# A decoder layer on one core: a product that alternates between two kinds of head, an earlier load, other buffer starts and other due times

## The chip, the cores and the metric

The kernel runs on one core of one Trainium2 chip. A run's time is the device time of the launch in microseconds (us). Three runs of the kernel before took 3005.85, 3009.3 and 3020.05 us, a median of 3009.3 us. The profile is of one more execution, of 3014.2 us.

## The reference

One layer of a decoder, in fp32, over 2048 tokens of width 1024: an RWKV-7 mixer with 16 heads of 64, a layer norm, an FFN of width 2816 with a causal convolution of width 3 and a gate, and a second layer norm.

```python
r = xr @ w_rkv[0]; k = xk @ w_rkv[1]; v = xv @ w_rkv[2]      # token shift mixes x and its predecessor
decay = exp(-exp(-softplus(-(w0 + tanh(xw @ w1) @ w2)) - 0.5))
a = sigmoid(a0 + (xa @ a1) @ a2); gate = sigmoid(xg @ g1) @ g2
def step(state, inp):                                         # for each of 2048 tokens, 16 heads, 64 x 64
    sa = einsum('bhij,bhj->bhi', state, -kk_t)
    state = state * w_t + sa x (kk_t * a_t) + v_t x k_t
    return state, einsum('bhij,bhj->bhi', state, r_t)
x = layer_norm(ALPHA * x + ((head_norm(y) + bonus) * gate) @ w_o)
hdn = conv(x @ w_in) + conv_b;  u, g = split(hdn)
out = layer_norm(ALPHA * x + (silu(g) * u) @ w_out)
```

## The kernel before

Four stages follow each other and overlap a little at their seams: the projections (0 to about 715 us, `a_nodes`), the recurrence (about 695 to 1285 us, `s_nodes`), the output projection with the first norm (about 1275 to 1520 us, `w_nodes`), and the FFN with the second norm (about 1500 us to the end, `f_nodes`).

**Large products.** A product of the projections, the output projection or the FFN is made of three TensorE matmuls of 128x512: each operand is split into a rounded part (H) and the rest (L), and HH, HL and LH are accumulated (`mm3`, L162 to L164 in the profile). In the names, `ps<-WH,xiH` reads: into `ps`, from the moving tile `WH` (512 columns) and the stationary tile `xiH` (128x128). In the FFN `ps<-xH,wiH` has x moving and the weights stationary, and `acc<-woH,aH` is the second product. Each matmul loads its stationary tile anew, beside the matmul ahead of it.

**Buffers.** Each pool is wrapped in `Pool64`, which rounds a tile's size in each partition up to 64 bytes. Where a tile begins in its partition, in bytes modulo 256, follows from the sizes of what lies in front of it. In the built program the large products' tiles begin at these remainders:

| matmuls | moving tile at | stationary tile at |
|---|---|---|
| projections, second column half (h=1): 1152 | 32 | 32 |
| projections, first column half (h=0): 1152 | 224 | 32 |
| FFN, first product: 4224 | 160 | 224 |
| FFN, second product: 2064, by the buffers | 32 | 32 or 224 |
| of these the last of the last block | 224 | 224 |

**Recurrence.** The 2048 steps are done in 16 chunks t of 128 tokens, each of two halves c of 64. Heads go in eight pairs p of two (e = 0, 1), which lie in partitions 0 to 63 and 64 to 127. For a chunk, loads (`th`, `rk`, `bk`), decays (`csI`, `P`, `Pi`), transposes (`tr`, `tb`, `pcp`) and Gram products `G` come first; DVE masks them into `Gm`. Part of `Gm` goes to DRAM (`NU`) and comes back as `NUs`; a table of identities comes from DRAM as `XU`; on these, DVE solves 32x32 triangular systems in 31 pairs of instructions (`itmp` and `XU`, L976 and L981), in place. `mp` merges two 32x32 solutions into one of 64x64. The part that goes from half to half is: `Z` (from `UV`, `Gm` and `state`), ACT copies it to `Zs`, `SA`, ACT copies it to `UV`, `dS`, then DVE forms `stmp` and `state` (L1129, L1134). `Z`'s second step (`f_z2`) has two matmuls for each pair p: one for e=1 that reads `state` and uses a 64x64 corner of the array, and one for e=0 that reads `SZ` and uses 128 rows and 64 columns. Before, the eight of the first kind come ahead of the eight of the second. From t=12 on the pairs are taken in two groups of four. These matmuls are in full fp32 and each shows as two passes in the profile (256 matmuls of a kind, 512 rows).

**Order.** All work is handed to a list scheduler (`Plan`). Each node has an engine, an estimated duration, a due time (`prio`, the smaller first), the nodes that it needs, and buffer slots. The plan writes down one order for each engine, and an engine runs its instructions in that order, waiting at the first that isn't ready. Due times are offsets in the tables `TS` (recurrence) and `TW` (output projection): for a chunk t, `b = t * T`, and `hs`, `cs`, `lds`, `inv` and so on are added to it. All loads named here go through SyncE's one DMA queue (SP).

Of the kernel before, what the change touches and what calls it, by code (L numbers as in the profile page):

```python
# [11 lines left out]
F32 = mybir.dt.float32  # L12
# [8 lines left out]
T, D, FF = 2048, 1024, 2816  # L21
# [11 lines left out]
    return bass.AP(tensor=ap.tensor, offset=ap.offset, ap=[[0, n], [1, ap.shape[-1]]])  # L33


class Pool64:


    def __init__(self, pool):
        self.pool = pool  # L40

    def tile(self, shape, dtype, **kw):
        n = math.prod(shape[1:])
        if n % 16 == 0:
            return self.pool.tile(shape, dtype, **kw)
        x = self.pool.tile([shape[0], -(-n // 16) * 16], dtype, **kw)[:, 0:n]
        if len(shape) > 2:
            d = " ".join(f"d{i}" for i in range(1, len(shape)))
            x = x.rearrange(f"p ({d}) -> p {d}", **{f"d{i}": shape[i] for i in range(2, len(shape))})
        return x  # L50
# [84 lines left out]
class K:  # L135
# [3 lines left out]

    def pool(self, st, **kw):  # L140
        p = st.enter_context(self.tc.tile_pool(**kw))
        return p if kw.get("space") is not None else Pool64(p)

    def ld(self, out, in_):
        return self.nc.sync.dma_start(out, in_)  # L145
# [1 line left out]
    st = ld  # L147
# [18 lines left out]
    def rsqrt(self, pool, out, x, n, m=None):  # L166

        nc = self.nc
        w = pool.tile([128, n], F32, name="rsw", bufs=1)[:, 0:m or n]
        y = pool.tile([128, n], F32, name="rsy", bufs=1)[:, 0:m or n]  # L170
        nc.vector.tensor_scalar(w.bitcast(I32), x.bitcast(I32), 1, None, op0=OP.arith_shift_right)
        nc.vector.tensor_scalar(y.bitcast(I32), w.bitcast(I32), -1.0, float(0x5F3759DF), op0=OP.mult, op1=OP.add)
        for i in range(3):
            nc.vector.tensor_tensor(w, y, y, op=OP.mult)
            nc.vector.scalar_tensor_tensor(w, w, -0.5, x, op0=OP.mult, op1=OP.mult)
            nc.vector.scalar_tensor_tensor(out if i == 2 else y, w, 1.5, y, op0=OP.add, op1=OP.mult)


    def run(self, phases="ASWF", scratch=None):
        tc, nc, a = self.tc, self.nc, self.a  # L180
        with ExitStack() as ctx:
            dram = ctx.enter_context(tc.tile_pool(name="dram", bufs=1, space=DRAM))
            self.S = {}
            mk = scratch or (lambda shape, name: dram.tile(shape, F32, name=name))
            for t in range(NT):
                for q in ("vc", "Y"):
                    self.S[q, t] = mk([128, D], f"{q}_{t}")
                self.S["gs", t] = mk([128, 2, D], f"gs_{t}")
                for h in range(2):

                    s = mk([129, 5, 512], f"in_{t}_{h}")
                    self.S["in", t, h] = s[1:129]
                    for i, q in enumerate(("r", "kkn", "b", "kp", "th")):
                        self.S[q, t, h] = s[0:128, i] if q == "kkn" else s[1:129, i]
                    self.S["kk0", t, h] = s[128:129, 1]
                    c = slice(h * 512, h * 512 + 512)
                    for q in ("vc", "Y"):
                        self.S[q, t, h] = self.S[q, t][:, c]
                    self.S["gateg", t, h] = self.S["gs", t][:, 0, c]
                    self.S["svbg", t, h] = self.S["gs", t][:, 1, c]  # L200
            self.x1T = [dram.tile([128, KD, 512], F32, name=f"x1T_{b}") for b in range(T // 512)]
            self.xn1 = [dram.tile([128, D], F32, name=f"xn1_{t}") for t in range(NT)]
            self.NU = [dram.tile([64, 1024], F32, name=f"NU_{t}") for t in range(NT)]
            self.XD = [dram.tile([64, 1024], F32, name=f"XD_{t}") for t in range(NT)]
            top = ctx.enter_context(tc.tile_pool(name="top", bufs=1))

            self.ident = top.tile([128, 136], F32, name="ident")[:, 8:136]
            self.ld(self.ident, a["c_ident"])
            self.build(ctx, phases)
            for n in self.plan.order():  # L210
                n.fn()

    def build(self, ctx, phases):
        ctx.enter_context(self.tc.manual_schedule())
        fs = {**self.TW["slots"], **self.TF["slots"]}
        fa = dict(self.TA["slots"])
        for h in range(2):
            fa.update({f"W{h}{k}": 1 for k in range(KD)})
        pl = self.plan = Plan({**fa, **self.TS["slots"], **fs}, fifo={*fa, *fs} - {"pg0", "pg1"})
        n_1, n_2 = self.a_nodes(ctx, pl) if "A" in phases else (None, None)  # L220
        pl.off = self.TS["p0"] + 23 * self.TA["g"] if "A" in phases else 0.0
        if "S" in phases:
# [6 lines left out]
    def a_nodes(self, ctx, pl):  # L229
# [56 lines left out]
        for sw, (q, wi, mm, ml) in enumerate((("k", 1, 2, 4), ("r", 0, 0, 1), ("v", 2, 3, 5))):  # L286
# [271 lines left out]
            for nq, (g, h, tl) in enumerate(order):  # L558
# [190 lines left out]
        return n_1, n_2  # L749


    TS = dict(hf=12, T=23.2, lds=5.0, hs=8.9, inv=31.0, mrg=66.3, mc=4.0, uv=47.5, st=70.2, cs=17.6, e0=30.0, p0=-3.4, fill=(), fn=1,
              slots=dict(cs=1, lth=1, lrk=1, lbk=1, pw=4, P=1, Pi=1, AR=4, BKn=4, Gm=4, PC=4, BKT=2, NUs=2, XU=2, XT0=1, XT1=1, X11=2, mp=1,
                         FT=2, UV=2, c0=1, c1=1, Y=1, Yt=1))

    def s_nodes(self, ctx, pl, n_1, n_2, w, f):

        tc, nc, a = self.tc, self.nc, self.a
        o = self.TS
        sl = o["slots"]  # L760
# [51 lines left out]
        inv = wkp = ldp = pw = triI = gmask = cols = gm4 = nbI = nbIn = nbE = scE = None  # L812
        cst = wk = ch2 = sm = pm = pc = None
        chs, XTs, SV, ZS, SW, V, SZ, n_za = [None] * sl["AR"], [], {}, {}, {}, {}, [], []
        n_o1 = pl.add("-", 0, 0, f_open1, [n_1])
        n_o2 = pl.add("-", 0, 0, f_open2, [n_o1, n_2])
        n_z2 = pl.add("POOL", 4.0, -9.0, f_zero2, [n_o2], lat=0.2)
        n_c = pl.add("SP", 2.0, -8.5, f_c, [n_o1])

        def tile_of(t, name, pool, shape, **kw):  # L820
            V[t][name] = pool.tile(shape, F32, name=name if isinstance(name, str) else name[0], **kw)
            return V[t][name]

        prevS, prevA, prevY = [], None, None
        for t in range(NT):
            v = V[t] = {}
            b = t * o["T"]
            P = lambda off, b=b: b + off
            grams, pcs, ars = [], [], {}
            for h in range(2):  # L830
                hb = b + h * o["hs"]
# [15 lines left out]
                n_lt = pl.add("SP", 1.0, lb - 0.3, f_lt, [n_o1], take=("lth",), lat=2.5)  # L847
# [2 lines left out]

                def f_cs(t=t, h=h):
                    MM(tile_of(t, ("csI", h), pw, [128, 512], tag="pw"), triI, V[t]["th", h])
                n_ci = pl.add("PE", 0.86, hb, f_cs, [n_lt] + [n_c] * (t == 0), take=("cs", "pw"), give=("lth",))

                def f_P(t=t, h=h):
                    P = tile_of(t, ("P", h), wkp, [128, 2, 512], tag="P", bufs=sl["P"])
# [7 lines left out]
                            nc.scalar.activation(x[es(part), c], V[t]["csI", h][es(c)], AF.Exp, bias=nbIn[es(c)],  # L864
                                                 scale=CDEC)
                n_P = pl.add("ACT", 1.24, hb + 0.2, f_P, [n_ci], take=("P",))
                n_Pi = pl.add("ACT", 2.4, hb + 0.4, f_Pi, [n_ci, n_P], take=("Pi",), give=("cs", "pw"))

                def f_alloc(t=t):
                    tile_of(t, "AR", chs[t % len(chs)], [128, 2, 8, 2, 64])  # L870
# [77 lines left out]
            e0 = (t == 0) * o["e0"]  # L948
            ib = b + o["inv"] - e0
# [15 lines left out]
                self.ld(x.rearrange("q m t -> q (m t)"), a["c_xui"])  # L965
            n_nu = pl.add("SP", 2.0, ib, f_nu, grams, lat=2.5)
            n_ns = pl.add("SP", 1.0, ib, f_nus, [n_nu], take=("NUs",), lat=3.0)
            n_xu = pl.add("SP", 1.0, ib, f_xu, [n_nu], take=("XU",), lat=2.5)
            prev = [n_ns, n_xu]
            for s in range(31):  # L970
                m, n = s // 2 + 1, 31 - s
# [21 lines left out]
            for c in range(2):  # L993
                mc = mb + o["mc"] * c
# [46 lines left out]
                n = pl.add("DVE", 0.93, mc, f_x11, [n_xt], take=("X11",))  # L1041
                n_m1 = pl.add("PE", 0.62, mc, f_m1, [n], take=("mp",), give=("X11",))
                n = pl.add("ACT", 0.79, mc, f_ft, [n_m1], take=("FT",), give=("mp",))
                n = pl.add("PE", 0.62, mc, f_m2, [n], take=("mp",), give=("FT",))
# [10 lines left out]
            for c in range(2):  # L1055
# [22 lines left out]
                for u in range(nh):  # L1078
                    ps = range(8 // nh * u, 8 // nh * (u + 1))
# [18 lines left out]
                    def f_z2(t=t, c=c, ps=ps, H=H, i0=i0):  # L1098
                        for p in ps:
                            MM(H["Z"][64:128, p], V[t]["AR"][64:128, c, p, 0], SV[i0][64:128, p], start=False,  # L1100
                               stop=p == ps[-1])
                        for p in ps:
                            MM(H["Z"][0:64, p], V[t]["AR"][:, c, p, 0], SZ[0][:, p], start=False, stop=p == ps[-1])

                    def f_zs(H=H, sl8=sl8, u=u, i0=i0):
# [25 lines left out]
                    def f_s1(t=t, c=c, u=u, sl8=sl8, i0=i0, i1=i1, n=ps[-1] + 1 - ps[0]):  # L1131
                        if u == 0:
# [15 lines left out]
                              give=("AR", "BKn", "Gm", "PC", "UV") if c else ())  # L1148
# [16 lines left out]
        for t0, t1, dt in o["fill"]:  # L1165
            n = pl.add("-", 0, 0, lambda: None, lat=t0)
            for i in range(int((t1 - t0) / dt)):
                pl.add("PE", 0.22 * o["fn"], 500 + i, f_fill, [n], take=("mp",), give=("mp",))
                n = pl.add("-", 0, 0, lambda: None, [n], lat=dt)
        if w:  # L1170
# [1 line left out]
                         pl.add("-", 0, 0, pools2.close, stores), stores, f)  # L1172


    TW = dict(ne=4, st=-31.5, gt=-31.1, tr=-14.5, ld=-22.0, out=26.9, p0=1000.0,
              slots=dict(w_ygE=2, w_gsE=2, w_yg=3, w_gs=4, w_xt=4, w_q=4, w_y=2, w_pwE=1, w_pwL=3, w_pzE=3, w_pzL=1,
                         w_xn=2, w_xo=2, w_st=2))

    def w_nodes(self, ctx, pl, n_first, n_ch1, xds, Q, n_rest, stores, f):

        tc, nc, a = self.tc, self.nc, self.a
        o = self.TW
        sl = {k[2:]: v for k, v in o["slots"].items()}
# [255 lines left out]
    def f_nodes(self, ctx, pl, Q, n_early, n_w, n_rest, zs, gn, n_sx, n_x1):  # L1439
# [51 lines left out]
        TAG = {"pz": "z", "pw": "tr"}  # L1491
        bank = lambda kind, i: kind + ("E" if i % 4 < self.TW["slots"][f"w_{kind}E"] else "L")
        pu = [0]
# [303 lines left out]
```

## Time and profile before

| | |
|---|---|
| median of 3 runs | 3009.3 us (3005.85 to 3020.05) |
| profiled execution | 3014.2 us, of which the span of the trace 3012.4 us |
| mean granted TensorE clock | 0.976 |
| TensorE busy | 2878.5 us (96%) |
| VectorE busy | 2018.5 us (67%) |
| ScalarE busy | 1693.5 us (56%) |

Busy shares are means over the four stages; in each of them another engine can be near its limit. A matmul's busy time in the profile is modelled, and neighbours overlap: what a matmul costs in a stream is the distance from its start to the next one's start. Rows that merge several instructions show how many (x16) and the start of the first.

### The profile page before, as it was taken

The numbers are of one execution on the slowest core, as the hardware profiler recorded it, in microseconds if no ns is written. First come the engines' busy times: TensorE is split into PE (matmuls) and PEld (weight loads), VectorE is DVE, ScalarE is ACT, GpSimd is POOL, SyncE is SP. The second block draws the span as 40 slices with busy tenths as digits, with TensorE's granted clock in tenths as the row PEclk, the third lists the DMA queues.
The fourth block names the chain that finished last, engine by engine and source line by source line (L and its number), as shares of the span: only waits on it lengthen the run. The fifth ranks groups of instructions, "written<-read, shape, count | busy, mean of one in ns | idle before, by whom it ended". The sixth has DMA issues, their size and how long they took to land.

```text
span 3012.4 us, 53465 instructions
## 1 busy us (share of the span) xinstructions
PE 2878.5 (96%) x20416; PEld 2342.4 (78%) x20416; DVE 2018.5 (67%) x4032; ACT 1693.5 (56%) x4580; POOL 53.5 (2%) x95
## 2 busy tenths in 40 slices
PE   7998999998899989989999999999999999999997
PEld 5776778886677877868888887878888788887886
DVE  7888769976877878678765555474554745547454
ACT  8888657655666766667554444434444344443441
POOL 0000000001000000001100000000000000000000
PEclk9999999999899999899999999999999999999999
DMA  6346555336666766468552334343243432434322
GB/s 204 138 165 232 174 182 195 142 117 178 158 154 155 173 156 142 127 229 284 191 182 89 95 97 124 96 143 96 88 126 95 144 95 89 133 95 143 91 84 81
DMA packets 283313, 428.12 MB, mean 142 GB/s; under 512 B 122448, under 2 KB 148048, under 8 KB 283056
## 3 DMA queue, kind: packets, MB, share of 16 engines
q1 hardware_dynamic: 271728, 383.81, 42.7%
q0 software_dynamic: 11328, 40.90, 3.7%
q8 instruction: 160, 2.62, 0.4%
q14 instruction: 97, 0.79, 0.1%
HBM read 315.50 MB, written 109.12 MB: 141 GB/s over the span
## 4 chain that ended last, share of the span: by engine, by line
issue 55%; PE 24%; ACT 7%; DMA 6%; DVE 6%; POOL 1%; SPq 1%; POOLq 0%; DVEq 0%; ACTq 0%
PE ps L162 4%; PE ps L163 4%; PE ps L164 4%; ACT junk L641 3%; PE Z L766 2%; DMA XU<-in_c_xui_dram 2%; PE G L766 1%; PE Y L766 1%; SPq L145 1%; PE csI L766 1%; ACT Pi L864 1%; DVE itmp L976 1%; DMA stg<-in_w_rkv_dram 1%; DVE XU L981 1%; PE dS L766 1%
## 5 line engine op out<-in xcount | busy, mean ns | idle before, releaser
L162 PE MATMUL ps<-xH,wiH 128*128 128x512 f32 x1408 | 557.2, 396 | 0.0
L164 PE MATMUL ps<-xH,wiL 128*128 128x512 f32 x1408 | 556.7, 395 | 0.5 <-DVE wiL L1585 0.3
L163 PE MATMUL ps<-xL,wiH 128*128 128x512 f32 x1408 | 556.6, 395 | 0.0
L1585 DVE TENSOR_TENSOR wiL<-wis,wiH 128x1024 fp32r<-128x1024 f32 x176 | 215.3, 1223 | 497.6 <-ACT wiH L1446 497.6
L1446 ACT ACTIVATE hb<-ps 128x512 f32<-128x512 f32 x176 | 105.6, 600 | 523.2 <-PE ps L164 523.2
L162 PE MATMUL ps<-WH,xiH 128*128 128x512 f32 x768 | 307.2, 400 | 15.6 <-ACT xiH L253 10.1
L164 PEld LDWEIGHTS ps<-xH,wiL 128*128 128x128 f32 x1408 | 264.7, 188 | 65.3 <-DVE wiL L1585 1.8
L163 PEld LDWEIGHTS ps<-xL,wiH 128*128 128x128 f32 x1408 | 264.9, 188 | 63.5
L162 PEld LDWEIGHTS ps<-xH,wiH 128*128 128x128 f32 x1408 | 264.8, 188 | 62.6
L163 PE MATMUL ps<-WL,xiH 128*128 128x512 f32 x768 | 304.7, 397 | 2.0 <-DVE WL L348 2.0
L164 PE MATMUL ps<-WH,xiL 128*128 128x512 f32 x768 | 304.4, 396 | 0.0
L163 PE MATMUL acc<-woL,aH 128*128 128x512 f32 x688 | 272.2, 396 | 9.8 <-DVE woL L1550 9.8
L1613 DVE SCALAR_TENSOR_TENSOR cv<-hb,cw,cv 128x512 f32<-128x512 f32 x352 | 263.6, 749 | 21.9 <-ACT cv L1609 15.7
L164 PE MATMUL acc<-woH,aL 128*128 128x512 f32 x688 | 272.1, 396 | 0.0
L162 PE MATMUL acc<-woH,aH 128*128 128x512 f32 x688 | 269.8, 392 | 0.0
L1446 ACT ACTIVATE wiH<-wis 128x1024 fp32r<-128x1024 f32 x178 | 189.0, 1062 | 11.9 <-DMA wis<-in_w_in_dram 11.9
L162 PEld LDWEIGHTS ps<-WH,xiH 128*128 128x128 f32 x768 | 146.5, 191 | 55.7 <-ACT xiH L253 10.1
L1446 ACT ACTIVATE woH<-wos 128x512 fp32r<-128x512 f32 x172 | 108.3, 632 | 123.5 <-PE acc L164 121.1
L163 PEld LDWEIGHTS ps<-WL,xiH 128*128 128x128 f32 x768 | 146.5, 191 | 35.0 <-DVE WL L348 2.5
L164 PEld LDWEIGHTS ps<-WH,xiL 128*128 128x128 f32 x768 | 146.1, 190 | 33.6 <-DVE xiL L472 0.2
L163 PEld LDWEIGHTS acc<-woL,aH 128*128 128x128 f32 x688 | 130.1, 189 | 42.0 <-DVE woL L1550 12.5
L976 DVE TENSOR_TENSOR itmp<-XU,NUs 128x126 f32<-128x126 f32 (+21 forms) x496 | 119.6, 252 | 55.3 <-DMA XU<-in_c_xui_dram 45.3
(244 smaller groups left out, 5294.2 us busy)
## 6 DMA issues: line engine op xcount, KB each, us to landing
wis<-in_w_in_dram SPq DMA_DIRECT2D x176, 512.0 KB
wos<-in_w_out_dram SPq DMA_DIRECT2D x172, 256.0 KB
xT<-in_xT_dram SPq DMA_DIRECT2D x21, 1028.0 KB
in<-kp SPq DMA_DIRECT2D x64, 256.0 KB
rk<-in SPq DMA_DIRECT2D x32, 512.0 KB
bk<-in SPq DMA_DIRECT2D x64, 256.0 KB
stg<-in_w_rkv_dram SPq DMA_DIRECT2D x48, 256.0 KB
gs<-gs SPq DMA_DIRECT2D x24, 512.0 KB
```

Source lines behind the costliest of these rows:

```text
L145: return self.nc.sync.dma_start(out, in_)
L162: nc.tensor.matmul(ps, lH, rH, start=start, stop=False)
L163: nc.tensor.matmul(ps, lH, rL, start=False, stop=False)
L164: nc.tensor.matmul(ps, lL, rH, start=False, stop=stop)
L641: nc.scalar.activation(junk, Z["kr"][:, 64 * i:64 * i + 64], AF.Square, accum_out=st["ss"][:, tl, i:i + 1])
L766: MM = lambda out, l, r, **kw: nc.tensor.matmul(out, l, r, **{**dict(start=True, stop=True), **kw}, skip_group_check=True)
L864: nc.scalar.activation(x[es(part), c], V[t]["csI", h][es(c)], AF.Exp, bias=nbIn[es(c)], scale=CDEC)
L976: TT(V[t]["tv"], V[t]["XU"][:, 0:m, s:s + 1].to_broadcast([128, m, n]), V[t]["NUs"][:, s:s + 1, s + 1:32].to_broadcast([128, m, n]), op=OP ...
L981: TT(x, x, V[t]["tv"], op=OP.add)
L1446: CP = lambda out, in_, **kw: nc.scalar.activation(out, in_, AF.Copy, **kw)
L1585: TT(W["L"], W["s"], W["H"], op=OP.subtract)
L1613: STT(R[j], W["hb"][:, i:i + 512], C["cw"][:, fc, i:i + 1], R[j], op0=OP.mult, op1=OP.add)
```

## The change

1. In `f_z2` the two matmuls of a pair p now follow each other, so that the kinds alternate eight times.
2. The load of `XU` (identities) needs only that its pool is open, and is due 12 units earlier. Before, it needed `NU`'s store, and so the Gram products.
3. `Pool256` takes the place of `Pool64`. It rounds sizes so that the buffers of one tile all begin alike modulo 256, and `ident` begins 64 bytes later in its tile, which is 64 bytes longer. In the built program every 128x512 matmul of the large products then has its stationary and its moving tile at remainder 224.
4. Other numbers in `TS` and `TW`, and two other estimated durations (`n_ci`, `n_Pi`).

```diff
-class Pool64:
+class Pool256:
-    def __init__(self, pool):
-        self.pool = pool
-    def tile(self, shape, dtype, **kw):
+    def __init__(self, pool, bufs):
+        self.pool, self.bufs = pool, bufs
+    def tile(self, shape, dtype, bufs=None, **kw):
+        b = bufs or self.bufs
         n = math.prod(shape[1:])
-        if n % 16 == 0:
-            return self.pool.tile(shape, dtype, **kw)
-        x = self.pool.tile([shape[0], -(-n // 16) * 16], dtype, **kw)[:, 0:n]
+        u = 64 // math.gcd(64, 16 * b) * 16 if n % 64 else 64
+        if n % u == 0 or n % 64 == 0:
+            return self.pool.tile(shape, dtype, bufs=b, **kw)
+        x = self.pool.tile([shape[0], -(-n // u) * u], dtype, bufs=b, **kw)[:, 0:n]
...
-            self.ident = top.tile([128, 136], F32, name="ident")[:, 8:136]
+            self.ident = top.tile([128, 152], F32, name="ident")[:, 24:152]
...
-    TS = dict(hf=12, T=23.2, lds=5.0, hs=8.9, inv=31.0, mrg=66.3, mc=4.0, uv=47.5, st=70.2, cs=17.6, e0=30.0, p0=-3.4, fill=(), fn=1,
+    TS = dict(hf=12, T=26.16, lds=5.61, hs=9.77, inv=31.0, mrg=66.3, mc=4.0, uv=47.5, st=70.2, cs=20.21, e0=30.0, p0=-3.4, fill=(), fn=1,
...
-            n_xu = pl.add("SP", 1.0, ib, f_xu, [n_nu], take=("XU",), lat=2.5)
+            n_xu = pl.add("SP", 1.0, ib - 12, f_xu, [n_o1], take=("XU",), lat=2.5)
...
                         for p in ps:
                             MM(H["Z"][64:128, p], V[t]["AR"][64:128, c, p, 0], SV[i0][64:128, p], start=False,
                                stop=p == ps[-1])
-                        for p in ps:
                             MM(H["Z"][0:64, p], V[t]["AR"][:, c, p, 0], SZ[0][:, p], start=False, stop=p == ps[-1])
...
-    TW = dict(ne=4, st=-31.5, gt=-31.1, tr=-14.5, ld=-22.0, out=26.9, p0=1000.0,
+    TW = dict(ne=4, st=-23.31, gt=-28.94, tr=-23.33, ld=-22.89, out=30.7, p0=1000.0,
```

The first place is TensorE's order around `f_z2` in the first half of chunk 5 (`Z<-state` and `Z<-SZ` are its two kinds; a row with x8 is eight matmuls in a row). Before:

```order
3096 L766 MATMUL Z<-UV,Gm 64x64 x16
3097 L766 MATMUL Y_11063<-UV,Gm 64x64 x16
3098 L766 MATMUL Z<-state,AR 64x64 x8
3099 L766 MATMUL Z<-SZ,AR 64x64 x8
3100 L766 MATMUL mp<-X_11260,Gm 32x32 x16
3101 L766 MATMUL Y_11307<-state,AR 64x64 x16
```

And after, at the same place, the start of the block and its end:

```order
3235 L768 MATMUL Y_11264<-state,AR 64x64 x16
3236 L768 MATMUL Z<-state,AR 64x64
3237 L768 MATMUL Z<-SZ,AR 64x64
3238 L768 MATMUL Z<-state,AR 64x64
3239 L768 MATMUL Z<-SZ,AR 64x64
...
3251 L768 MATMUL Z<-SZ,AR 64x64
3252 L768 MATMUL mp<-XT_7824,FT 32x32 x16
3253 L768 MATMUL SA<-Zs,XT_7824 64x64 x16
```

Two runs of eight became sixteen single matmuls of changing kind; `Y<-state` moved from behind the block to ahead of it, and 16 `mp` stand between the block and `SA`.

The second place is SyncE's queue in one chunk of the recurrence, around the loads of `NUs` and `XU` (`NU_163` is that chunk's table in DRAM; `bk`, `rk` and `th` are loads for a later chunk). Before:

```order
461 L145 DMA rk<-in_0_95 128x1024
462 L145 DMA XT_7827<-XD_177 32x8x32 x4
463 L145 DMA XT_7828<-XD_177 32x8x32 x4
464 L145 DMA th<-in_0_100 128x512
465 L145 DMA NU_163<-Gm 32x16x32 x4
466 L145 DMA UV<-vc_82 64x1024 x2
467 L145 DMA NUs<-NU_163 64x1024 x2
468 L145 DMA XU<-in_c_xui_dram 128x512
```

After:

```order
459 L147 DMA XT_7824<-XD_177 32x8x32 x4
460 L147 DMA XU<-in_c_xui_dram 128x512
461 L147 DMA bk<-in_0_95 64x2x512 x2
462 L147 DMA XT_7825<-XD_177 32x8x32 x4
463 L147 DMA rk<-in_0_95 128x1024
464 L147 DMA th<-in_1_96 128x512
465 L147 DMA UV<-vc_82 64x1024 x2
466 L147 DMA NU_163<-Gm 32x16x32 x4
467 L147 DMA bk<-in_1_96 64x2x512 x2
468 L147 DMA NUs<-NU_163 64x1024 x2
```

`XU` moved from just behind `NUs` to six rows ahead of `NU`'s store; one load of `bk` now stands between that store and `NUs`.

The third place is TensorE's order at the seam to the output projection, where `tr<-ident,wE` are its first transposes. Before:

```order
3437 L766 MATMUL Y_17025<-state,AR 64x64 x16
3438 L766 MATMUL SA<-Zs,XT_7828 64x64 x8
3439 L766 MATMUL Z<-state,AR 64x64 x4
3440 L766 MATMUL Z<-SZ,AR 64x64 x4
3441 L1329 MATMUL tr<-ident,wE 128x128 x4
3442 L766 MATMUL dS<-UV,BKn 64x64 x8
```

After:

```order
3855 L768 MATMUL Y_16813<-UV,Gm 64x64 x16
3856 L768 MATMUL Z<-UV,Gm 64x64 x8
3857 L1330 MATMUL tr<-ident,wE 128x128 x4
3858 L768 MATMUL Z<-state,AR 64x64
3859 L768 MATMUL Z<-SZ,AR 64x64
3860 L768 MATMUL Z<-state,AR 64x64
```

The first transposes moved ahead of the last chunk's `f_z2`.

## Rows read from the trace of the kernel before

**Rows 1.** The page's head: span of the trace.

```profile
span 3012.4 us, 53465 instructions
```

**Rows 2.** Busy time by stretch: length, PE, PEld, DVE, ACT, POOL, clock, DMA.

```profile
0.00:700.00 700.00, 667.99 (x3097) 532.26 (x3098) 563.63 (x1158) 510.61 (x1846) 3.93 (x13) 0.98 0.51 173
797.00:1164.00 367.00, 334.21 (x6800) 285.81 (x6796) 291.26 (x911) 243.22 (x497) 5.87 (x11) 0.96 0.66 157
1164.00:1290.00 126.00, 111.04 (x2377) 98.11 (x2377) 91.95 (x304) 83.51 (x232) 5.90 (x11) 0.88 0.51 131
1500.00:2000.00 500.00, 499.53 (x2163) 403.74 (x2162) 275.14 (x367) 237.62 (x466) 4.25 (x6) 1.00 0.36 111
```

**Rows 3.** Waits of PE from 740 to 1290 us: total, times, longest.

```profile
PE Z L766 <- DVE stmp L1129: 10.5, 11, 2.1
PE csI L766 <- DVE Gm L944: 5.7, 3, 3.7
...
PE tb L926 <- DVE itmp L976: 2.2, 1, 2.2
```

**Rows 4.** Timeline of PE, 943 to 948 us: start, duration, line, tile, form, count.

```profile
943.36 1.15 PE L766 MATMUL Z<-UV,Gm 64*64 64x64 f32 x32
944.43 1.15 PE L766 MATMUL Y<-UV,Gm 128*64 128x64 f32 x32
945.52 1.14 PE L766 MATMUL Z<-state,AR 64*64 64x64 f32 x16
946.59 1.15 PE L766 MATMUL Z<-SZ,AR 128*64 128x64 f32 x16
947.66 0.50 PE L766 MATMUL mp<-X,Gm 32*32 32x32 f32 x20
```

**Rows 5.** Timeline of PE, 932.20 to 932.38 us: the block's first two passes.

```profile
932.26 0.33 PE L766 MATMUL Z<-state,AR 64*64 64x64 f32 x2
```

**Rows 6.** Timeline of PE, 933.20 to 933.45 us: the switch from one kind to the other.

```profile
933.01 0.39 PE L766 MATMUL Z<-state,AR 64*64 64x64 f32 x4
933.33 0.33 PE L766 MATMUL Z<-SZ,AR 128*64 128x64 f32 x2
```

**Rows 7.** Instructions that write Z: duration ns min/median/max, first and last start.

```profile
L766 PE MATMUL Z<-state,AR x512: 218/218/366, 745.4 to 1278.7; 64*64 64x64 f32 x171
```

**Rows 8.** Timeline of PE, projections: first and last of two blocks of 24.

```profile
305.04 0.39 PE L162 MATMUL ps<-WH,xiH 128*128 128x512 f32 x1
...
310.25 0.39 PE L164 MATMUL ps<-WH,xiL 128*128 128x512 f32 x1
...
310.93 0.39 PE L162 MATMUL ps<-WH,xiH 128*128 128x512 f32 x1
...
316.30 0.39 PE L164 MATMUL ps<-WH,xiL 128*128 128x512 f32 x1
```

**Rows 9.** Timeline of PE, FFN: first and last of one block of 24.

```profile
1707.81 0.40 PE L162 MATMUL ps<-xH,wiH 128*128 128x512 f32 x1
...
1713.18 0.39 PE L164 MATMUL ps<-xH,wiL 128*128 128x512 f32 x1
```

**Rows 10.** Timeline of PE, second products: a (32, 32) run, a (224, 224) run.

```profile
2008.72 0.39 PE L162 MATMUL acc<-woH,aH 128*128 128x512 f32 x1
...
2011.89 0.39 PE L164 MATMUL acc<-woH,aL 128*128 128x512 f32 x1
...
2980.36 0.39 PE L162 MATMUL acc<-wiH,aH 128*128 128x512 f32 x1
...
2982.17 0.39 PE L164 MATMUL acc<-wiH,aL 128*128 128x512 f32 x1
```

**Rows 11.** Waits of DVE from 740 to 1290 us.

```profile
DVE itmp L976 <- DMA XU<-in_c_xui_dram: 38.7, 12, 6.7
```

**Rows 12.** Timeline of SP, 885 to 925 us: one chunk's two loads.

```profile
916.25 1.10 SPq L145 DMA_DIRECT2D NUs<-NU  x2
917.39 1.10 SPq L145 DMA_DIRECT2D XU<-in_c_xui_dram  x1
```

More of the change, by code (lines that the diff above doesn't have):

```diff
@@ L141, in pool @@
         p = st.enter_context(self.tc.tile_pool(**kw))
-        return p if kw.get("space") is not None else Pool64(p)
+        return p if kw.get("space") is not None else Pool256(p, kw["bufs"])
     def ld(self, out, in_):
@@ L852, in f_cs @@
                     MM(tile_of(t, ("csI", h), pw, [128, 512], tag="pw"), triI, V[t]["th", h])
-                n_ci = pl.add("PE", 0.86, hb, f_cs, [n_lt] + [n_c] * (t == 0), take=("cs", "pw"), give=("lth",))
+                n_ci = pl.add("PE", 1.06, hb, f_cs, [n_lt] + [n_c] * (t == 0), take=("cs", "pw"), give=("lth",))
                 def f_P(t=t, h=h):
@@ L866, in s_nodes @@
                 n_P = pl.add("ACT", 1.24, hb + 0.2, f_P, [n_ci], take=("P",))
-                n_Pi = pl.add("ACT", 2.4, hb + 0.4, f_Pi, [n_ci, n_P], take=("Pi",), give=("cs", "pw"))
+                n_Pi = pl.add("ACT", 2.79, hb + 0.4, f_Pi, [n_ci, n_P], take=("Pi",), give=("cs", "pw"))
                 def f_alloc(t=t):
```

## The prediction

> **What bounds the kernel now.** I read the busy time by stretch first, since the page's means cover four stages. In the FFN TensorE is busy for 499.53 of 500 us, DVE for 275 and ACT for 238; in the projections TensorE is busy for 668 of 700 us [rows 2]. There the time is the number of matmuls times the distance from one start to the next, and nothing else. In the middle of the recurrence (797 to 1164 us, eleven chunks at 33.4 us each) TensorE is busy for 334 of 367 us and DVE for 291: TensorE is nearly full, and DVE is close behind. The waits of TensorE come next: the largest is for `stmp`, 10.5 us in 11 waits, then 5.7 us for `Gm` and 2.2 us for `itmp`, all three on DVE [rows 3]. Added TensorE work there is largely visible, but some can go into these waits. Last I read timelines of TensorE, for what one matmul costs in a stream.
>
> **Alternating kinds in Z.** A block of eight pairs now takes 947.66 - 945.52 = 2.14 us, half for each kind [rows 4]. Its parts can be taken apart. The first two passes end 0.33 us after the start, and one pass is 0.218 us long, so the second starts 0.11 us after the first [rows 5, 7]. From the fourth pass before the change of kind to the change it is 933.33 - 933.01 = 0.32 us, which is three steps and one change; a whole half (1.07 us) is that first step of 0.11, 14 further steps and one change [rows 4, 6]. The difference, 1.07 - 0.11 - 0.32 = 0.64 us, is 11 steps: 0.058 us a step, and so 0.147 us for a change of kind. When the kinds alternate, each single matmul is two passes, 0.11 us apart, and then a change: sixteen times 0.257 us, or 4.11 us, against 2.14. That is +1.97 us for a full block. For a group of four pairs it is 8 x 0.257 = 2.06 us against 2 x (0.11 + 6 x 0.058 + 0.147) = 1.21, or +0.85. Chunks 0 to 11 have 24 full blocks and chunks 12 to 15 have 16 groups: 24 x 1.97 + 16 x 0.85 = +61 us of TensorE time.
>
> There is an opposite reading. `Z<-UV` has 32 passes that alternate between corners of one size, and takes 944.43 - 943.36 = 1.07 us, no more than 16 passes of one kind [rows 4]. If the two kinds of `f_z2` ran side by side like that, a block would fall to 1.07 us, and the sum would be 24 x -1.07 + 16 x -0.6 = -35 us. But `Z<-UV` stays within 64x64, and here 64x64 alternates with 128x64. The change at 933.33 is just this pair of kinds, on disjoint parts of the array, and it cost 0.147 us [rows 6]. I take the loss.
>
> [...]
>
> How much of the 61 us shows? TensorE's idle time is 367 - 334 = 33 us in the middle and 126 - 111 = 15 us in the tail, 48 us together [rows 2]. At best all of it takes up the new work: then 13 us show. At worst none does: 61 us. The waits on DVE come to 18 us by the three largest rows [rows 3], and with TensorE slower DVE catches up; the order also has more TensorE work standing ahead of a block (`Y<-state` moved there). I let 27 of the 48 us be taken up, a little over half: **+34 us**.
>
> **Buffers alike modulo 256.** The same matmul has two speeds in this trace. In the projections a block with both tiles at remainder 32 goes from 305.04 to 310.25 us, 23 distances of 226.5 ns; the next block, with the moving tile at 224 and the stationary one at 32, goes from 310.93 to 316.30, 233.5 ns [rows 8]. The FFN's first product (160 and 224) has 1713.18 - 1707.81 = 5.37 us, 233.5 ns again [rows 9]. In the second product a run at (32, 32) has (2011.89 - 2008.72) / 14 = 226.4 ns, and the few matmuls that are at (224, 224) already have (2982.17 - 2980.36) / 8 = 226.3 ns [rows 10]. So it isn't the remainder but whether the two agree. After the change all agree at 224. FFN: 4224 x 7.0 ns = -29.6 us, all of it on the path, since TensorE is never idle there [rows 2]. Projections, h=0: 1152 x 7.0 ns = -8.1 us, of which I count half, since this stage has 32 us of idle TensorE that can grow. The second product's runs start anew at each block and I count them at nothing. 29.6 + 4 is 33.6, less a little for runs that start anew: **-33 us**. The bounds: 0, if the start of a stream decides and not the remainder; -42 us with the whole of the projections and 4 us from the second product, which is 2 ns on each of its 2064.
>
> [...]
>
> **Identity ahead of the Gram products.** DVE waits 38.7 us in 12 waits for `XU` [rows 11], but `XU` is issued at 917.39, right where `NUs`, issued at 916.25 for 1.10 us, ends [rows 12]. Both are needed, so the wait turns to `NUs`, and at most one issue is gained: 12 x 1.1 = 13 us, on an engine that TensorE waited for directly only for 2.2 us (`itmp`) [rows 3]. In the new order one load of `bk` stands between `NU`'s store and `NUs`, which costs about as much again. Bounds -13 and +13, and I take **-2 us**. Queued behind the earlier `XU` are `bk`, `rk` and `th` of a later chunk; its buffers are long free, so it holds nothing up.
>
> **Offsets and seam.** The new numbers fill other places with the same work. The first transposes of the output projection now come ahead of the last chunk's `f_z2`; the tail has 15 us of idle TensorE to win, at a granted clock of 0.88 [rows 2]. An order that puts a late instruction first can lose as much. Bounds -15 and +10, and I take **-4 us**. Moving `ident` I cost at nothing: only transposes read it, and none of the terms above does.
>
> **Sum.** The profiled execution has 3014.2 us, of which 3012.4 is span [rows 1] and 1.8 lies around it. 3014.2 + 34 - 33 - 2 - 4 = 3009.2. That execution was 4.9 us above the median of the three runs, so the forecast for a median is 3004 us. A change of 0.5% (15 us) is about what a measurement can tell from none: below 2994 is faster, above 3024 slower.
>
> **Rivals.**
> - *The new order covers the drains.* For it: 48 us of idle, most of it on DVE. Against it: the idle is spread over many short waits (2.1 us at most for `stmp`), and 4.11 us sit in the chain from `state` to `Zs`. Then only 13 us show: 3014.2 + 13 - 33 - 6 - 4.9 = 2983 us.
> - *Slower: the drained block sits on the chain from half to half.* `state`, `Z`, `Zs`, `SA`, `UV`, `dS`, `stmp`, `state` is serial, and each half now carries 2 us more. It decides as soon as the work set beside the block is shorter than the chain: then TensorE's waits stay as they are, all 61 us show, and the seam and `XU` give nothing back: 3014.2 + 61 - 33 - 4.9 = 3037 us. For it: TensorE already waits for `stmp` in 11 blocks. Against it: those waits are short, and TensorE has other work.
> - *The spacing doesn't come.* Remainder and place in the program go together in the rows, and the start of a stream could be what counts. 3014.2 + 34 - 6 - 4.9 = 3037 us. Against it: four different pieces of code agree with the remainders.
> - *No drain.* The kinds run side by side: 3014.2 - 35 - 33 - 6 - 4.9 = 2935 us. [...]
>
> **How the numbers follow.** The forecast has 0.50, with a range of its own from 2988 to 3022; covered drains 0.18; drains on the chain 0.19; no new spacing 0.06; no drain 0.07. Faster takes 0.18 + 0.07 and 0.08 of the forecast's lower end, 0.33. Slower takes the two cases at 3037 less their lower edge, 0.24. The rest, 0.43, is no change. The range from 2965 to 3038 leaves out the case without drains and about half of those at 3037.
>
> **What would show it.** Of each step: `Z<-state` and `Z<-SZ` as single pairs of passes with 0.26 us from kind to kind, and 4.1 us for a block; chunks of 35 to 37 us in place of 33.4; an FFN block of 24 with 5.21 us from first to last start in place of 5.37, and FFN and norm together about 30 us shorter; DVE's wait named `NUs`, hardly shorter. Wrong would be: blocks of about 1.1 us; FFN blocks that stay at 5.37 us; a chunk of 33 us or less in spite of drained blocks, or one over 37.5 us.

## The result: slower by 0.7%

| | us |
|---|---|
| before, median of 4 runs | 3012.95 (3005.85 to 3020.05) |
| after, median of 4 runs | 3036.24 (3033.54 to 3040.26) |
| after / before, by the record | 1.0069, 95% interval 1.0048 to 1.0089 (the two medians alone give 1.0077) |
| profiled execution of after, span of its trace | 3031.7 |

The forecast was 3004 us, no change. The time lies at the upper end of the whole range (2965 to 3038 us) and outside the forecast's own (2988 to 3022 us), and the direction is wrong. The page of after, its head and the granted clock in 40 slices of the span:

```profile
span 3031.7 us, 53483 instructions
PE 2933.6 (97%) x20416; PEld 2407.5 (79%) x20416; DVE 2021.6 (67%) x4032; ACT 1697.9 (56%) x4580; POOL 53.2 (2%) x95
PEclk9999999999887888979999999999999999999999
```

TensorE is busy for 55 us more than before, and the clock row has a dent of 7 and 8, with one 9 in it, from slice 11 to slice 18 (about 758 to 1364 us, 76 us each), which is the recurrence. By stretch (columns as in [rows 2]):

```profile
0.00:700.00 700.00, 664.89 (x3116) 535.80 (x3117) 567.68 (x1162) 514.71 (x1862) 3.94 (x13) 0.98 0.52 173
797.00:1164.00 367.00, 357.99 (x5904) 297.73 (x5902) 252.87 (x774) 214.15 (x432) 5.34 (x10) 0.85 0.57 137
1164.00:1290.00 126.00, 123.40 (x2208) 102.91 (x2202) 95.62 (x312) 75.18 (x163) 3.21 (x6) 0.91 0.56 130
1500.00:2000.00 500.00, 499.58 (x2239) 413.41 (x2239) 282.97 (x408) 242.61 (x509) 9.38 (x13) 1.00 0.37 118
```

From 797 to 1164 us TensorE's idle time fell from 33 us [rows 2] to 9, as hoped, and yet it passed fewer instructions in that stretch, 5904 against 6800, at a granted clock of 0.85 against 0.96. The projections and the FFN go the other way: 2239 matmuls against 2163 in the same 500 us.

Where the time went, by first and last starts of the stages: projections 5 us shorter; from the first `Z<-state` to the last `dS` 610 us in place of 537, **+73**; from there to the last `z` 206 in place of 224, -18; from the first to the last of the FFN's first products, with second products in between, 1393.0 in place of 1420.4, **-27**.

Blocks of `f_z2` at full clock, and one at half clock (timeline of TensorE):

```profile
788.36 0.33 PE L768 MATMUL Z<-state,AR 64*64 64x64 f32 x2
788.61 0.33 PE L768 MATMUL Z<-SZ,AR 128*64 128x64 f32 x2
788.87 0.32 PE L768 MATMUL Z<-state,AR 64*64 64x64 f32 x2
...
792.47 1.15 PE L768 MATMUL Y<-state,AR 64*64 64x64 f32 x32
...
947.83 2.07 PE L768 MATMUL G<-AR,BKT 64*128 64x128 f32 x14 [1.59 <-ACT Pi L866]
949.83 0.47 PE L768 MATMUL Z<-state,AR 64*64 64x64 f32 x2
950.23 0.47 PE L768 MATMUL Z<-SZ,AR 128*64 128x64 f32 x2
950.63 0.47 PE L768 MATMUL Z<-state,AR 64*64 64x64 f32 x2
```

At full clock a block takes 792.47 - 788.36 = 4.11 us, 0.255 us from kind to kind, exactly as worked out from [rows 4 to 7]. The change of kind is worth 0.147 us in it, and that is all that the traces show of what the prediction calls a drain; what the array does in that time no run shows. In the second one it is 0.40 us from kind to kind: the granted clock is 0.50 there (950 to 960 us). Ahead of that block it had stood still for 1.59 us, but the stretch from 930 to 940 us, just behind another block, is at half clock as well, and there TensorE is never idle:

```profile
930.00:940.00 10.00, 10.00 (x170) 8.98 (x168) 1.11 (x4) 4.19 (x11) 0.00 (x0) 0.50 0.46 107
```

Waits from 740 to 1290 us, TensorE's largest and DVE's:

```profile
PE G L768 <- ACT Pi L866: 5.7, 5, 1.7
...
PE Z L768 <- DVE stmp L1130: 1.0, 2, 0.8
```

```profile
DVE stmp L1130 <- PE dS L768: 78.4, 22, 8.9
DVE Gm L946 <- PE G L768: 37.2, 18, 5.4
...
DVE itmp L978 <- DMA NUs<-NU: 5.3, 4, 4.0
```

The wait for `stmp` went from 10.5 us [rows 3] to 1.0, and DVE now waits for TensorE. In the middle the recurrence is bound by TensorE, idle for 9 us in 367, and the wait of 38.7 us for `XU` [rows 11] is gone, with 5.3 us left on `NUs`.

In a block of 24 of the projections' first half and one of the FFN, the answers to [rows 8, 9]:

```profile
311.09 0.39 PE L164 MATMUL ps<-WH,xiH 128*128 128x512 f32 x1
...
316.30 0.39 PE L166 MATMUL ps<-WH,xiL 128*128 128x512 f32 x1
```

```profile
1709.02 0.39 PE L164 MATMUL ps<-xH,wiH 128*128 128x512 f32 x1
...
1714.23 0.39 PE L166 MATMUL ps<-xH,wiL 128*128 128x512 f32 x1
```

Both have 5.21 us for 23 distances, 226.5 ns, where they had 5.37.

### The profile page after: what moved, and what is told of

It is laid out like the page before. It is cut to its first block, busy times and chain, and to the rows that moved or that the text cites. A ratio compares the mean times of both kernels' runs of the same rounds, so it can differ in the third digit from the quotient of the medians.

```text
span 3031.7 us, 53483 instructions
## 1 busy us (share of the span) xinstructions
PE 2933.6 (97%) x20416; PEld 2407.5 (79%) x20416; DVE 2021.6 (67%) x4032; ACT 1697.9 (56%) x4580; POOL 53.2 (2%) x95
## 4 chain that ended last, share of the span: by engine, by line
issue 54%; PE 30%; ACT 7%; DVE 5%; DMA 3%; POOL 1%; SPq 0%; POOLq 0%; DVEq 0%; ACTq 0%
PE Z L768 5%; PE ps L164 4%; PE ps L165 4%; PE ps L166 4%; ACT junk L643 3%; PE Y L768 2%; PE G L768 2%; PE SA L768 2%; PE mp L768 1%; PE dS L768 1%; PE tr L901 1%; DMA in<-av 1%; PE csI L768 1%; PE tb L928 1%; ACT Pi L866 1%
## 5 line engine op out<-in xcount | busy, mean ns | idle before, releaser
L166 PE MATMUL ps<-xH,wiL 128*128 128x512 f32 x1408 | 548.2, 389 | 0.5 <-DVE wiL L1586 0.5
L164 PE MATMUL ps<-xH,wiH 128*128 128x512 f32 x1408 | 548.2, 389 | 0.0
L165 PE MATMUL ps<-xL,wiH 128*128 128x512 f32 x1408 | 547.8, 389 | 0.0
L164 PEld LDWEIGHTS acc<-woH,aH 128*128 128x128 f32 x688 | 130.2, 189 | 27.9 <-ACT woH L1447 0.7
```

The costliest lines, as they stand in the source:

```text
L164: nc.tensor.matmul(ps, lH, rH, start=start, stop=False)
L165: nc.tensor.matmul(ps, lH, rL, start=False, stop=False)
L166: nc.tensor.matmul(ps, lL, rH, start=False, stop=stop)
```

## The experiments

Two theories at first: the alternation costs all of the loss and more (A), or the earlier load and the new order do (B). Half-clock time is the length of a stretch times 2 x (1 - granted clock), added up over 720 to 1360 us in pieces of 10 us, of which none has a granted clock under 0.50 in any of these traces; before has 99 us by that count and after 191. It comes from one profile of each kernel. Ten executions of before on one chip have granted clocks from 0.973 to 0.980 over the whole kernel, which is 163 to 120 us at half clock, so a difference of some 40 us between two profiles shows nothing by itself. The last column therefore has the granted clock of all runs; after has 0.958 to 0.960. The ratios are against the kernel before on the same chip.

| kernel | median us | ratio (95%) | half clock, us | clock of the runs |
|---|---|---|---|---|
| e1, after with two runs of eight | 2954.4 | 0.9801 (0.9779 to 0.9823) | 71 | 0.977 to 0.982 |
| e2, before with the alternation | 3071.9 | 1.0193 (1.0165 to 1.0222) | 147 | 0.962 to 0.970 |
| e4, e1 with full-array filler | 2977.3 | 0.9876 (0.9856 to 0.9895) | 58 | 0.982 to 0.985 |
| e5, before with Pool256 | 2982.0 | 0.9895 (0.9874 to 0.9916) | 93 | 0.971 to 0.977 |
| e6, before with the early XU | 2990.6 | 0.9928 (0.9904 to 0.9952) | 78 | 0.977 to 0.980 |
| e7, before with the new offsets | 3001.8 | 0.9959 (0.9944 to 0.9975) | 120 | 0.974 to 0.981 |
| e8, after with full-array filler | 3059.6 | 1.0153 (1.0127 to 1.0180) | 138 | 0.964 to 0.971 |
| e9, e1 with other remainders | 2961.9 | 0.9828 (0.9810 to 0.9846) | 82 | 0.978 to 0.979 |
| e10, after in groups of two | 2981.9 | 0.9861 (0.9815 to 0.9906) | 102 | 0.969 to 0.976 |
| e11, e1 with the old offsets | 2960.9 | 0.9799 (0.9767 to 0.9830) | 99 | 0.974 to 0.977 |

**e1: the alternation undone.**

```diff
                                stop=p == ps[-1])
+                        for p in ps:
                             MM(H["Z"][0:64, p], V[t]["AR"][:, c, p, 0], SZ[0][:, p], start=False, stop=p == ps[-1])
```

> The changed kernel with one part undone: in f_z2 the eight matmuls of one kind stand ahead of the eight of the other again, as before. Theory A (the alternation costs twice: 61 us of TensorE time for the changes of array size, of which some goes into idle time, and then a lower granted clock, since the recurrence's half-clock time rose from 95 to 191 us between the two traces): the time falls to 2970 to 2990 us, half-clock time of 720 to 1360 us goes back under 120 us, and chunks take 32 to 34 us. Theory B (the earlier XU load and the new offsets made the recurrence longer, the alternation is hidden in TensorE's idle time): the time stays above 3020 us and chunks stay above 36 us.

2954.4 us, better than both kernels, and below the range expected: the other three parts together are worth -59 us, not the -39 forecast for them. The alternation costs 3036.2 - 2954.4 = **82 us** beside them (81 by the ratios). The order of DVE's and ACT's work in its trace is that of after, instruction for instruction, and TensorE's too but for these blocks, so nothing else changed. Theory B falls. In its trace and that of after, the whole recurrence (from just at its first `Z` to its last `dS`):

```profile
L768 PE MATMUL dS<-UV,BKn x1024: 222/222/370, 783.7 to 1268.2; 128*64 128x64 f32 x171
740.00:1270.00 530.00, 482.56 (x9648) 416.31 (x9647) 425.16 (x1327) 358.90 (x789) 10.15 (x19) 0.94 0.65 157
```

```profile
L768 PE MATMUL dS<-UV,BKn x1024: 222/222/369, 784.5 to 1347.9; 128*64 128x64 f32 x171
740.00:1350.00 610.00, 587.11 (x9639) 485.36 (x9638) 424.32 (x1322) 358.87 (x792) 10.18 (x19) 0.85 0.56 136
```

The same instructions take TensorE 482.6 us busy in the one and 587.1 in the other, 104.5 us more, and its idle time falls from 47.4 to 22.9. So 24.5 us were taken up (27 were forecast), and of the 104.5 the changes of array size, at full clock, are 61. That leaves 44 us, which the clock accounts for: 530 x 2 x 0.06 = 64 us at half clock against 610 x 2 x 0.15 = 183, 119 us more. At half clock a single matmul of the block takes 0.40 us in place of 0.255, 1.57 times as long; at that rate 119 us do what 76 us do at full clock, and 43 are lost. This is an estimate: for other matmuls the factor is larger (in after the 32 passes of `dS` from 821.93 us take 1.15 us at full clock and those from 937.00 us 1.98 at half, the last pass being 0.222 and 0.369 of it, so 30 and 52 ns from pass to pass, 1.74 times), and by that 51 us would be lost. In the sum, 61 - 24.5 + 44 = 80.5 against the 82, the 44 is what the busy time leaves.

**e2: the alternation alone**, on the kernel before.

```diff
-                        for p in ps:
                             MM(H["Z"][0:64, p], V[t]["AR"][:, c, p, 0], SZ[0][:, p], start=False, stop=p == ps[-1])
```

> The kernel before with the alternation in f_z2 alone. Theory A: about 61 us of TensorE work less what idle time takes up, plus the fall of the clock: +50 to +80 us, 3060 to 3090 us, with blocks of 4.1 us at full clock. Theory B: within 15 us of before.

3071.9 us, +58 us, as theory A expected. Here too the sum closes: the recurrence is 56 us longer, TensorE's busy time in it 81 us more, which is 61 for the changes of size and, at 50 us more of half clock, 18 to 21 for the clock by the same two factors, and its idle time 24 us less. It is less than 82 us because half-clock time rises by 48 us here and by 120 there. Why it rises less under the old order no run shows.

**e4: as much TensorE work, but on the full array.** On top of e1; the added product is overwritten.

```diff
                         H["Z"] = pc.tile([128, 8, 64], F32, name="Z", tag=f"c{H['u']}")
+                        for _ in range(8 if len(ps) == 8 else 0):
+                            MM(H["Z"][:, 0:2].rearrange("q p i -> q (p i)"), triI, gmask)
```

> The changed kernel with f_z2 in two runs of eight, as before, and in chunks 0 to 11 eight added matmuls of 128x128 on constants ahead of each full block's Z (their result is overwritten): about the same added TensorE time per block, 2.0 us, but in full-array matmuls without a change of size between them. If the granted clock fell because the alternating block leaves the array idle most of the time (theory A), the clock here stays as before (under 120 us at half clock) and the time is 10 to 35 us above that of the kernel with two runs of eight. If the clock falls with any added TensorE work, or from the new order, it is again near 190 us at half clock and the time is near 3030 us.

In its trace the filler and what follows it, and the middle of the recurrence:

```profile
906.85 2.05 PE L768 MATMUL Z<-c_gmask,c_triI 128*128 128x128 f32 x16
908.84 1.15 PE L768 MATMUL Z<-UV,Gm 64*64 64x64 f32 x32
```

```profile
797.00:1164.00 367.00, 353.28 (x6898) 310.09 (x6896) 279.73 (x855) 234.68 (x473) 5.86 (x11) 0.98 0.63 151
```

1.99 us per block, within 0.02 us of what the alternation adds to one (4.11 - 2.14 = 1.97), 24 times: 48 us of work cost 23 us of time, at a clock of 0.98. So the same occupied time was cheap here in full-array matmuls, and dear where the array size changes: in this stretch the clock is at 0.85 with the alternation (after; 0.94 in e2, under the old order), and neither added work of this kind (0.98) nor the new order without it (e1, 0.95) shows such a fall. The 16 groups of four carry no filler here, so it is 48 us to set beside 61. No run added dense work on a part of the array, so whether it is fullness that counts, or that the size stays the same, is not told apart.

**e8: the same filler on top of after.**

> The changed kernel, with the alternation, and the eight full-array matmuls on constants ahead of each full block's Z (chunks 0 to 11; their result is overwritten): 24 times 1.99 us of added TensorE work, 48 us. Clock theory: the added full-array work brings the granted clock back up in part, half-clock time falls from 191 us to 150 us or less, and the time rises by far less than 48 us (under +25 us over 3036). If the clock does not respond: +40 us or more, since TensorE has almost no idle time left in the recurrence.

```profile
797.00:1164.00 367.00, 359.84 (x5932) 303.90 (x5931) 241.20 (x749) 200.55 (x403) 4.80 (x9) 0.91 0.53 127
```

TensorE had 9 us of idle in this stretch, and 48 us of added work over all cost 23.4 us: the clock went from 0.85 to 0.91, and the half-clock time from 191 to 138 us (over the whole recurrence, which ends behind 1360 us here, from 188 us in 610 to 147 in 635). The four runs have a clock of 0.964 to 0.971 against 0.958 to 0.960, so this isn't the scatter of one profile: full-array work brought the clock back up in part.

**e10: half as many changes of size.**

```diff
-                        for p in ps:
-                            MM(H["Z"][64:128, p], V[t]["AR"][64:128, c, p, 0], SV[i0][64:128, p], start=False,
-                               stop=p == ps[-1])
-                            MM(H["Z"][0:64, p], V[t]["AR"][:, c, p, 0], SZ[0][:, p], start=False, stop=p == ps[-1])
+                        for q in ps[::2]:
+                            for p in (q, q + 1):
+                                MM(H["Z"][64:128, p], V[t]["AR"][64:128, c, p, 0], SV[i0][64:128, p], start=False,
+                                   stop=p == ps[-1])
+                            for p in (q, q + 1):
+                                MM(H["Z"][0:64, p], V[t]["AR"][:, c, p, 0], SZ[0][:, p], start=False, stop=p == ps[-1])
```

> The changed kernel with f_z2 in groups of two: two matmuls of one kind, two of the other, and so on. A full block has 8 changes of size (the changed kernel 16, two runs of eight 2): 8 x (0.11 + 2 x 0.058 + 0.147), less one step's rounding, 2.98 us at full clock, +0.84 over two runs of eight, and a group of four pairs +0.28: +25 us of TensorE work over the kernel with two runs of eight (2954 us). If the cost were work alone, less what idle time takes up: 2964 to 2970 us. If the granted clock falls with the work's emptiness too, in proportion: half-clock time (720 to 1360 us) between 71 and 191, near 110 us, and 2975 to 2990 us. If the clock falls only when the kinds alternate singly: half-clock time at 80 us or less and 2964 to 2970 us.

2981.9 us (the runs scatter from 2968 to 2987), a ratio 0.006 above e1, or 18 us, with half clock between the two, 102 us. A block takes 2.99 us at full clock (870.39 to 873.38), as worked out. In the recurrence TensorE is busy for 35 us more than in e1 and idle for 11 us less. A clock that falls in proportion is not shown by this: 31 us of half clock are within the scatter of single profiles, before has 99 us without any of it, and the clock of the runs is near that of before on the same chip (0.971 to 0.979). By the time alone the reading without the clock (2964 to 2970) is not excluded either, since the interval is wide.

**Where the clock falls.** The traces of these runs show what TensorE did before each fall. Take the stretch of the full blocks, from the second to the last of the 24. In after the clock falls 16 times there, and 15 of the falls come in a block or less than 1 us behind its end, though the blocks with that 1 us make up 30% of the stretch. In e2 it is all 11 falls, in e8 12 of 14. With two runs of eight it is 2 of 8 in e1, 2 of 8 in e9, and none of the 29 falls in before, e4, e5, e6, e7 and e11; in groups of two (e10) it is 1 of 5. One of the blocks of after, and what follows it:

```profile
881.40:885.40 4.00, 4.00 (x36) 2.99 (x32) 3.83 (x9) 1.41 (x4) 0.53 (x1) 1.00 0.77 203
886.10:896.10 10.00, 10.00 (x170) 8.97 (x168) 2.33 (x10) 4.34 (x12) 0.00 (x0) 0.50 0.59 135
```

So in these traces the falls go with the single alternation (38 of 41, against 4 of 45 with two runs of eight), and not with added work as such. Not every block has one (15 of 23 in after, 11 of 23 in e2), and which of them do is open. A good part of the half clock thus falls on the work behind a block and not on the block.

**e5: Pool256 and the identity tile alone.** The first two parts of the diff shown with the change.

> The kernel before with Pool256 and the moved identity tile alone. If agreeing remainders set the distance between large matmuls: FFN 27 us shorter, projections 5 us shorter, 2976 to 2984 us, and the recurrence within 5 us of before. If the new buffer starts also slow the recurrence (other remainders for its tiles): the recurrence is more than 10 us longer and the time stays above 2990 us.

2982.0 us, -31.5 us. The profiled execution, 8 us faster than that median, has the stretch of the FFN's first products at 1388.1 us (1420.4 before), the projections 5 us shorter and the recurrence at 540 us (537). The term of -33 us holds. The mean distance of the first product falls from 233.2 to 226.7 ns, and that of the second product, which the sum had at nothing, from 229.5 to 226.8.

**e9: agreement or remainder?** On top of e1:

```diff
-            self.ident = top.tile([128, 152], F32, name="ident")[:, 24:152]
+            self.ident = top.tile([128, 136], F32, name="ident")[:, 8:136]
```

> The changed kernel with f_z2 in two runs of eight (2954 us) and the identity tile at its old size, which moves all buffers on one side by 64 bytes: FFN's first product and the projections' second column half are then at 160 for both tiles, the projections' first half at 224 (moving) and 160, the second product half at 224 and 160. If agreement counts, not the remainder: FFN's first product stays at 226.5 ns, the projections' first half goes to 229 to 233.5 ns, and the time is 3 to 12 us above 2954. If remainder 224 is what is fast: the FFN's first product goes back to 233 ns and the time to 2980 us or more.

A block of the projections at 224 (moving) and 160, then one of the FFN at 160 and 160:

```profile
309.82 0.40 PE L164 MATMUL ps<-WH,xiH 128*128 128x512 f32 x1
...
315.10 0.39 PE L166 MATMUL ps<-WH,xiL 128*128 128x512 f32 x1
...
1711.05 0.39 PE L164 MATMUL ps<-xH,wiH 128*128 128x512 f32 x1
...
1716.26 0.39 PE L166 MATMUL ps<-xH,wiL 128*128 128x512 f32 x1
```

229.6 and 226.5 ns. The FFN's first product keeps its speed at 160 once a block runs, and what no longer agrees loses 3 ns: here it is agreement that counts. But the block shown follows another of its own kind. Where a block of the first product follows one of the second product, which no longer agrees, its first ten distances have 230 ns on average and the rest 226.7, so that the first product as a whole has 227.9 ns (226.7 in e1, 233.2 before); the second product has 229.9 (226.8). The time is 7.5 us above e1, in the range expected, but all of it lies in the FFN (1399.6 us in place of 1392.1), while the projections, which were to give 3 ns in 1152 matmuls, are as long as in e1.

**e6: the early XU load alone.**

> The kernel before with the earlier load of XU alone. By the prediction's term (the wait passes to NUs and one issue of 1.1 us is gained 12 times at most): 0 to -13 us, near -2, and DVE's wait names NUs. If XU's late load had held the recurrence up by its whole 38.7 us of DVE waits: chunks 1 us or more shorter and 20 us or more off the time.

2990.6 us, -22.9 us: outside the 0 to -13 expected by the prediction's term, and in the range named for the other reading. The waits from 740 to 1290 us, DVE's and TensorE's:

```profile
DVE itmp L976 <- DMA NUs<-NU: 26.2, 10, 5.3
```

```profile
PE Z L766 <- DVE stmp L1129: 4.1, 4, 2.0
```

The wait did pass to `NUs`, and 38.7 - 26.2 = 12.5 us of it went, within the bound of 13. But the time fell by almost twice that. The recurrence is 25 us shorter in the profile (512 in place of 537): TensorE is idle in it for 38.3 us in place of 51.8, its waits for `stmp` (10.5 us before) and for `Gm` being shorter, and busy for 473.9 us in place of 485.5, as half-clock time is 27 us less there. The second part may be scatter: the runs' clock is 0.979 on average against 0.977 for before, which is 11 us of half clock in all and worth about 5 us. The order on the engines differs from that of before as well, so this run doesn't tell what the load gave and what the order did.

**e7 and e11: the offsets.** e7 has the `TS` and `TW` numbers and the two durations alone; e11 is e1 with the old ones.

> The kernel before with the new numbers in TS and TW and the two new durations alone. Undoing the alternation gave 2954, Pool256 alone 2982: 27 us are left for the XU load and the offsets. If the offsets carry them: 2980 to 2992 us, with the seam (last dS to last z) about 18 us shorter than the 224 us of before. If they only work together with the XU load: within 6 us of before.

> Pool256 and the early XU load, with f_z2 in two runs of eight and the old numbers in TS, TW and the two durations. The parts alone gave -31.5 us (Pool256) and -23 us (XU); if they add, 2957 to 2961 us, a few us slower than with the new offsets (2954). If the new offsets keep their -12 us beside the other two: 2964 to 2970 us.

Alone they give -11.8 us, between the two expectations. With these the alternation, Pool256, the load and the offsets, each alone, add up to +58 - 31.5 - 23 - 12 = -8 us, and together they are +23: the parts don't add. Beside the other parts the offsets give nothing that can be told: e11 has 0.9799 and e1 0.9801, with intervals that overlap almost wholly. The recurrence of e11 is 13 us shorter than that of e1 (516 against 529), and its seam from the last `dS` to the last `z` 17 us longer (223 against 206).

Both kinds of `f_z2` in one array size would remove even the last two changes; no run shows what that would give.

## Why the prediction was wrong, point by point

- *What bounds the kernel.* Right: the FFN by the distance between matmuls, the recurrence by TensorE with DVE close behind.
- *The price of the alternation, +61 us of TensorE time.* Right: 4.11 us a block. The rival in which the kinds run side by side, with blocks of about 1.1 us, is out.
- *How much of it shows, +34 us.* **This is the step that failed.** The idle time took up 24.5 us, close to the 27 forecast, but the rest was costed at full clock. The work was counted as time on an engine whose speed stays the same; it didn't, as the falls of the clock at the alternating blocks and e1, e4 and e8 show (0.85 from 797 to 1164 us in after, 0.95, 0.98 and 0.91 in these), and the lower granted clock added 44 us. The term measures +82 us beside the other parts and +58 us alone. The clock stood in the rows of before, 0.88 in the tail [rows 2], but no term of the sum let it move.
- *Buffers alike, -33 us.* Right: -31.5, and by agreement and not by remainder (e9). One part of the sum was missed: the second product gained 2.7 ns a matmul where it had none. The rival in which the new spacing doesn't come is out: the first product went from 233.2 to 226.7 ns.
- *Identity, -2 us.* Mis-sized: -22.9 us alone, outside its bounds of -13 and +13, and about as much on top of Pool256 (e5 to e11: -29 by the ratios, -21 by the medians, which are from two chips). The bound on DVE's own gain held, 12.5 us. What failed was to price DVE by the one wait of TensorE that names it (2.2 us): TensorE's idle time fell by 14 us in e6. That DVE's wait came back to TensorE under other names is the likely reading, but the order changed too, and the cause stays open.
- *Offsets and seam, -4 us.* Within its bounds: the seam is 18 us shorter in after, but the offsets are worth -12 us alone and about nothing beside the rest.
- *The sum.* By the medians -31.5 - 21 - 6.5 (e11 to e1, within their scatter) + 82 = +23 us. These are the steps from before over e5, e11 and e1 to after, so they come to the measured difference by construction. Against the forecast's 34 - 33 - 2 - 4 = -5 the alternation is 48 us dearer and the rest 20 us better.
- *The rivals.* The block on the chain from half to half gave 3037 us, and 3036 was measured, but that is not what happened: it had TensorE's waits stay as they are, and they fell from 33 to 9 us in the middle. Its time was right by luck: it left out what the clock cost and what the load gave, which offset each other in part.
- *What was to show it.* The block at 4.1 us, the FFN block at 5.21 and `NUs` in the wait's name all came, but the wait, forecast as hardly shorter, fell to 5.3 us. Chunks took 38.1 us (ten of them from the block at 788.4 to the one at 1169.4), beyond the 37.5 named as wrong.

## What to carry to other kernels

Before two small products are interleaved on TensorE, look whether they use the same array size: each change cost 0.147 us here, and a run of eight of one size paid it once. Cost added TensorE work twice, as time and by what it does to the granted clock: 2 us a block cost 23 us in all as full-array matmuls (e4), and some 80 as changes of array size. To find the cause of a fall, look at what TensorE did just before it. Where large matmuls are the bound, line up the starts of the moving and the stationary tile modulo 256 bytes: it gave 1% in this kernel.

## What the runs showed of the hardware that was not expected

- The granted clock fell while TensorE was busy for 358 of 367 us (0.85), and rose again when full-array matmuls were added (0.91), at the same kind of block. Two kernels with the same added TensorE time per block stood at 0.98 and 0.85. In the three kernels that alternate singly, 38 of 41 falls among the full blocks came in such a block or less than 1 us behind it.
- In the streams read here, once they run, a matmul of 128x512 followed the one before it at 226.3 to 226.7 ns where both tiles begin alike modulo 256, at 160 (e9) as at 224 (after) and at 32 (before). It was 233.5 ns where the moving tile begins 64 bytes below the stationary one (224 and 32, 160 and 224), and 229.6 ns where it begins 64 bytes above it (224 and 160). The first ten of a stream took 230 ns on average in spite of agreement (e9).
